# RWKV mixer: 128x128 matmuls over two heads in place of matmuls of 64 rows or columns

## Chip, cores and metric

The kernel runs on one core of one Trainium2 chip. The metric is device time in microseconds (us), the median of the runs.

## What is computed

A decoder trunk of two layers over 256 tokens of width 2048, in fp32: layer 0 mixes with window attention and a state-space scan, layer 1 with RWKV-7, and each is followed by a squared-ReLU MLP. The change lies in RWKV-7, which has 32 heads of 64 channels:

```python
def rwkv7_scan(r, w, k, v, a, b):
    def step(S, inp):
        r_t, w_t, k_t, v_t, a_t, b_t = inp
        sa = jnp.einsum('bhvk,bhk->bhv', S, a_t)
        S = S * w_t[:, :, None, :] + sa[..., None] * b_t[:, :, None, :] + v_t[..., None] * k_t[:, :, None, :]
        return S, jnp.einsum('bhvk,bhk->bhv', S, r_t)
...
    y = rwkv7_scan(rh, hs(decay), kh, vh, -kk, kk * ah)
    mu = jnp.mean(y, axis=-1, keepdims=True)
    var = jnp.mean(jnp.square(y - mu), axis=-1, keepdims=True)
    y = ((y - mu) * lax.rsqrt(var + GN_EPS)).reshape(b_, L, D)
    y = hs(y * ln_w.astype(jnp.float32) + ln_b.astype(jnp.float32))
    bonus = jnp.sum(rh * kh * r_k.astype(jnp.float32), axis=-1, keepdims=True) * vh
    y = (y + bonus).reshape(b_, L, D).astype(dt_)
    return (y * g) @ w_o.astype(dt_)
```

## The kernel before

Projections are made of 128-wide output tiles (units). Each fp32 weight is split into a rounded half (hi, ScalarE, L463) and the rest (lo, VectorE, L468); a k tile then takes three single-pass matmuls of 256 tokens, hi with the input's two halves and lo with the first (L494 to L496). They go to PSUM tiles named pu, from SA (values) or SB (keys and the output projection).

`mixer1` (L1202) handles 16 pairs of heads, one head on partitions 0 to 63 and one on 64 to 127. The 256 tokens are cut into 4 chunks of 64. The scan over tokens becomes products within a chunk, the inverse of a triangular matrix I - N, and a state carried over the chunks. For each pair j these stages run as generators:

- `prep_a` makes decay and gate and the scaled keys and queries, AR (ar, from the left) and bk.
- `prep_b` (L1363) multiplies bk by ar for each head (64 rows, 128 columns, fp32, 8 matmuls per pair) and masks the blocks into N (nt), ar and G; it sends the diagonal blocks of N through DRAM and transposes bk into bkn (8 transposes of 64 rows).
- `blocks`, `substitute` (GpSimd) and `levels` (32x32 matmuls, ps_i) make the inverse Y.
- `values` makes v and its transpose in uv (4 transposes of 128 rows to 64 columns).
- `chunks` (L1514) runs over 4 chunks, for both heads: the right side pr (L1527), from the second chunk on the state's part of the output (L1531), a copy rhs (VectorE), the inverse times it (L1543), the copy into uv (ScalarE), the state's update pS (L1553) and the output's other part (L1556), and the new state in uv (VectorE). Each is two matmuls, one per head, with the second head's result on partitions 64 to 127; the outputs are 64 wide.
- `finish` (L1566) does the group norm, transposes (4 of 128 rows to 64 columns), and multiplies by the gate on GpSimd.
- `keys`, `mixed`, `partial`, `whole` copy the projections' results and feed the output projection.

The order in which every engine gets its instructions is set by `Streams` (L200): it takes from all generators, the projections' among them, the operation that could start first by planned durations (`eP`, `eA`, `eD`, `eG`: TensorE, ScalarE, VectorE, GpSimd). `eW` names the events that a stage has to follow; with them the rings of buffers are kept. The third argument of `eP` is a shape: the time of the first load and of the last matmul. The numbers by which `Streams` chooses, and the order of the projections' parts, are in `PRM`. Each engine then executes its list in order and waits on semaphores where operands are late.

PSUM banks: pu 2, ps_a, ps_b, ps_i and ps_c one each, ps_y 2. AR has 4 buffers, KT 4 (and 3 in K3), bkn and G 3, bk 1, uv 2.

Of the kernel before, what the change touches and what calls it, by code (L numbers as in the profile page):

```python
# [13 lines left out]
P = 128  # L14
D = 2048
# [30 lines left out]
def _consts():  # L46
# [24 lines left out]
    c["blk32"] = (s64 // 32) == np.arange(2)[None, :]  # L71
# [10 lines left out]
for _k, _v in CONST.items():  # L82
    _l = int(_k in ("triu", "cos", "sin", "amask"))     # the second array serves layer 0 alone
    COFF[_k] = (_l, NCONST[_l], _v.shape[1])
    NCONST[_l] += _v.shape[1]


def _units(w):
    """[K, M] -> [M/128, 128, K/128, 128]"""
    k, m = w.shape  # L90
    return np.ascontiguousarray(w.reshape(k // P, P, m // P, P).transpose(2, 1, 0, 3))
# [6 lines left out]
def _heads(v):  # L98
    """a column to a head, on the first 64 partitions"""
    return np.concatenate([v.reshape(-1, HD).T, np.zeros((HD, D // HD), np.float32)], 0)  # L100


def layout(inp):
# [55 lines left out]
# ---------------------------------------------------------------- interleaving  # L159

WIDE, TILES, COLS, SMALL = (0.107, 0.107), (0.053, 0.02), (0.107, 0.002), (0.027, 0.02)


def eP(cost, after=None, shape=WIDE):
    """shape: the time to load the first stationary operand, which the matmul before hides, and the
    last matmul's time, which hides the next load"""
# [23 lines left out]
# the order of the parts of the projections and the weights by which Streams chooses  # L190
# [1531 lines left out]
```

## Time and profile before

| what | before |
| --- | --- |
| median of 3 runs | 2543.54 us (2540.68 to 2544.55) |
| span of the profiled execution | 2551.5 us (its own time is not listed beside it) |
| instructions | 45990 |
| TensorE busy, share of the span | 2477.5 us, 97% |
| VectorE | 1738.2 us, 68% |
| ScalarE | 1306.5 us, 51% |
| GpSimd | 527.2 us, 21% |
| mean granted clock of TensorE | 0.983 |

The span runs from the first to the last instruction of one profiled execution. PE is TensorE, PEld its weight loads, DVE VectorE, ACT ScalarE, POOL GpSimd. Matmuls are pipelined, so the busy times of two that overlap aren't a sum of costs; the distance of starts is. In tile names, out<-in, buffer numbers are left out. 64*64 64x64 means 64 rows and 64 columns of the array, an operand of 64 partitions and 64 elements. An fp32 matmul stands as two records, a transpose or a projection's matmul as one. The mixer's pairs run from about 1285 to 1760 us.

### The profile page before, as it was taken

What the parts mean: (1) busy time and instruction counts of PE and PEld (TensorE: products, weight loads), DVE (VectorE), ACT (ScalarE), POOL (GpSimd) and SP (SyncE); (2) the same over time, 40 slices, a digit from 0 to 9 for tenths busy, and PEclk for the clock granted to TensorE, in tenths of its full rate; (3) what the DMA queues carried; (4) which work ended last, traced back from release to release, by engine and by line L of the source; (5) the groups of instructions that cost most, each with busy time, mean ns of one, the idle gap of its engine ahead of it and who ended that gap; (6) DMA issues with size and microseconds to landing.
All of it is one profiled execution on the core that took longest, in us unless ns stands there. A gap on an engine that the chain in (4) does not pass through costs nothing. (4 is left out here: it accounts for less than half of the span.)

```text
span 2551.5 us, 45990 instructions
## 1 busy us (share of the span) xinstructions
PE 2477.5 (97%) x17612; PEld 2181.3 (85%) x17612; DVE 1738.2 (68%) x3287; ACT 1306.5 (51%) x2398; POOL 527.2 (21%) x933
## 2 busy tenths in 40 slices
PE   8999999999999999979999999999899999999999
PEld 7988988888888888879998888788688888888887
DVE  7888876656656656679876767667665565665665
ACT  5455555435445345556656566555453453453543
POOL 3443200000000000046455656552200000000000
PEclk9999999999999999989999999899999999999999
DMA  5433455555555555634442323334455555555554
GB/s 193 141 108 109 151 187 182 187 185 188 184 189 184 188 184 188 209 113 164 162 153 93 108 95 106 97 108 171 145 190 186 187 184 188 185 188 185 189 194 162
DMA packets 130348, 415.27 MB, mean 163 GB/s; under 512 B 23600, under 2 KB 26288, under 8 KB 130128
## 3 DMA queue, kind: packets, MB, share of 16 engines
q1 hardware_dynamic: 128160, 406.44, 46.9%
q0 software_dynamic: 1968, 5.90, 0.6%
q8 instruction: 138, 2.26, 0.3%
q14 instruction: 82, 0.67, 0.1%
HBM read 407.56 MB, written 4.72 MB: 162 GB/s over the span
## 5 line engine op out<-in xcount | busy, mean ns | idle before, releaser
L322 DVE TENSOR_TENSOR lo<-wt,hi 128x1024 fp32r<-128x1024 f32 (+2 forms) x895 | 937.4, 1054 | 529.6 <-ACT hi L319 511.8
L319 ACT ACTIVATE hi<-wt 128x1024 fp32r<-128x1024 f32 (+2 forms) x945 | 813.6, 873 | 818.3 <-PE pu L343 786.7
L343 PE MATMUL pu<-SA,hi 128*128 128x512 f32 (+2 forms) x4184 | 1162.0, 349 | 18.2 <-ACT SA L319 8.0
L343 PE MATMUL pu<-SB,hi 128*128 128x512 f32 (+2 forms) x3304 | 1003.1, 366 | 4.0 <-POOL SB L322 2.2
L343 PE MATMUL pu<-SA,lo 128*128 128x256 f32 (+1 forms) x3168 | 895.8, 283 | 0.3 <-DVE lo L322 0.3
L343 PEld LDWEIGHTS pu<-SA,hi 128*128 128x128 f32 (+1 forms) x4184 | 724.8, 191 | 135.2 <-ACT hi L319 9.7
L343 PE MATMUL pu<-SB,lo 128*128 128x256 f32 x2752 | 775.7, 282 | 1.7 <-DVE lo L322 1.6
L343 PEld LDWEIGHTS pu<-SB,hi 128*128 128x128 f32 (+1 forms) x3304 | 587.0, 190 | 115.6 <-POOL SB L322 2.6
L343 PEld LDWEIGHTS pu<-SA,lo 128*128 128x128 f32 (+1 forms) x3168 | 603.6, 191 | 1.2 <-DVE lo L322 0.5
L343 PEld LDWEIGHTS pu<-SB,lo 128*128 128x128 f32 x2752 | 522.6, 190 | 2.5 <-DVE lo L322 2.3
L1694 POOL DMA_DIRECT2D out<-xT x16 | 8.7, 544 | 708.0 <-DVE xT L322 708.0
L1661 POOL DMA_DIRECT2D xd<-xh x13 | 7.2, 554 | 696.5 <-DVE xh L322 696.5
L322 DVE TENSOR_TENSOR xh<-xh,pu 128x256 f32<-128x256 f32 x164 | 69.2, 422 | 53.7 <-PE pu L343 51.1
L322 DVE TENSOR_TENSOR xT<-xT,pu 128x256 f32<-128x256 f32 x154 | 64.8, 421 | 47.9 <-PE pu L343 45.3
L322 POOL TENSOR_TENSOR lo<-wt,hi 128x512 fp32r<-128x512 f32 (+1 forms) x50 | 69.1, 1387 | 66.3 <-ACT hi L319 62.2
L322 POOL TENSOR_TENSOR xt<-Nb,X 128x60 f32<-128x60 f32 (+14 forms) x240 | 74.7, 311 | 28.4 <-DMA Nb<-dn 12.1
L322 POOL TENSOR_TENSOR X<-X,xt 128x60 f32<-128x60 f32 (+14 forms) x240 | 74.2, 309 | 16.4
L319 ACT ACTIVATE uv<-ps_c,n 64x64 f32<-64x64 f32 x128 | 39.5, 309 | 53.0 <-PE ps_c L343 40.3
L322 POOL TENSOR_TENSOR SB<-st,SB 128x256 fp32r<-128x256 f32 x44 | 49.3, 1135 | 43.8 <-ACT SB L319 31.4
L340 DVE SCALAR_TENSOR_TENSOR uw<-u,rb 128x256 f32<-128x256 f32 x128 | 54.5, 425 | 4.4
L340 DVE SCALAR_TENSOR_TENSOR st<-dx,vec,xh 128x256 f32<-128x256 f32 x80 | 53.3, 700 | 2.0 <-POOL SB L322 2.0
L322 DVE TENSOR_TENSOR u<-pu,eb 128x256 f32<-128x256 f32 x128 | 53.6, 418 | 0.0
(310 smaller groups left out, 2073.2 us busy)
## 6 DMA issues: line engine op xcount, KB each, us to landing
wt<-in_w_up SPq DMA_DIRECT2D x256, 512.0 KB
wt<-in_w_dn SPq DMA_DIRECT2D x256, 512.0 KB
wt<-in_w_in SPq DMA_DIRECT2D x64, 512.0 KB
wt<-in_w_out SPq DMA_DIRECT2D x32, 512.0 KB
wt<-in_w_k SPq DMA_DIRECT2D x32, 512.0 KB
wt<-in_w_v SPq DMA_DIRECT2D x32, 512.0 KB
wt<-in_w_o SPq DMA_DIRECT2D x32, 512.0 KB
wt<-in_w_r SPq DMA_DIRECT2D x26, 512.0 KB
```

The costliest lines, as they stand in the source:

```text
L319: return self.nc.scalar.activation(out=out, in_=in_, func=func, **kw)
L322: return (eng or self.nc.vector).tensor_tensor(out=out, in0=a, in1=b, op=op)
L340: return self.nc.vector.scalar_tensor_tensor(out=out, in0=a, scalar=s, in1=b, op0=op0, op1=op1)
L343: return self.nc.tensor.matmul(out, lhsT, rhs, start=start, stop=stop)
L1661: spill = lambda d, e=nc.gpsimd: e.dma_start(out=xd[:, d, :], in_=x[d])
L1694: store = lambda d: nc.gpsimd.dma_start(out=ap["out"][:, d, :], in_=x[d])
```

## The change

In `chunks`, `prep_b`, `values` and `finish`, matmuls and transposes use all 128 rows and columns. AR holds for each head 128 columns: the scaled keys with what prep_b puts on the other half of the partitions, and the queries, with zeros elsewhere; one product (L1527's) then gives the right side on one half of the partitions and the state's part of the output on the other. BG holds the transposed bk and G together, so that a second product gives the state's update and the output's other part. `finish` adds the two parts of the output (R, the copy of the first product, and ps_y). Y becomes block diagonal over both heads, and one matmul of 128 columns replaces two. prep_b's 8 matmuls are issued head by head in turn into two banks. `Streams` gets a further number per shape, the rows, and plans 0.09 us where it changes. `_heads` repeats ln_w and ln_b on both halves. ps_b gets 2 banks, used in turns by prep_b and finish (`claim`), ps_y 1; AR 3 buffers, KT 3. `PRM` stays. Comments are removed; the diff shown leaves them out.

```diff
-WIDE, TILES, COLS, SMALL = (0.107, 0.107), (0.053, 0.02), (0.107, 0.002), (0.027, 0.02)
+WIDE, HALF, COLS, SMALL, ROWS = (0.107, 0.107, 128), (0.107, 0.053, 128), (0.107, 0.002, 128), (0.027, 0.02, 32), (0.107, 0.107, 64)
...
-            return max(self.free["P"] + max(0.0, load - self.tail), t + load - 0.07)
+            drain = 0.0 if op[3][2] == self.rows else 0.09
+            return max(self.free["P"] + drain + max(0.0, load - self.tail), t + load - 0.07)
...
-            AR = [wk.tile([P, 4, 3, HD], F32, name=f"AR{i}") for i in range(4)]
+            AR = [wk.tile([P, 4, 2, 2, HD], F32, name=f"AR{i}") for i in range(3)]
-            YY = [wk.tile([P, 4, HD], F32, name=f"YY{i}") for i in range(2)]
+            YY = [wk.tile([P, 4, 2, HD], F32, name=f"YY{i}") for i in range(2)]
+            for ar in AR:
+                for i in range(2):
+                    nc.gpsimd.memset(ar[H[1 - i], :, i, 1 - i, :], 0.0)
... prep_a
-                yield eW(("w", ("l", j, 0)), ("keys", j), ("chunks", j - 4), ("values", j - 2),
-                         ("finish", j - 4))
+                yield eW(("w", ("l", j, 0)), ("keys", j), ("values", j - 2), ("finish", j - 4))
...
+                yield eW(("chunks", j - 3))
...
-                yield eG(0.69, 0)
-                self.mul(ar[:, :, 1, :], v4(r), EE[:, :, 1:], nc.gpsimd)
+                for i in range(2):
+                    yield eG(0.69, 0)
+                    self.mul(ar[H[i], :, i, 1 - i, :], v4(r)[H[i]], EE[H[i], :, 1:], nc.gpsimd)
...
-                yield eG(0.69, t_kq)
-                self.mul(bk[:, :, 1, :], v4(kq), IE[:, :, 1:], nc.gpsimd)
+                for i in range(2):
+                    yield eG(0.69, t_kq)
+                    self.mul(bk[H[i], :, 1 - i, :], v4(kq)[H[i]], IE[H[i], :, 1:], nc.gpsimd)
... prep_b
+                turn = yield from claim()
+                pb = [PT("ps_b", 2) for _ in range(2)]
+                t_P = yield eP(0.9, None, ROWS)
+                for cc in range(4):
+                    for i in range(2):
+                        self.mm(pb[i][:, cc * P:(cc + 1) * P], bk[H[i], cc], ar[H[i], cc, i])
                 for i in range(2):
-                    ps = PT("ps_b")
-                    t_P = yield eP(0.87)
-                    for cc in range(4):
-                        self.mm(ps[:, cc * P:(cc + 1) * P], bk[H[i], cc, i:i + 2, :], ar[H[i], cc, i:i + 2, :])
...
-                for i in range(2):
-                    ps = PT("ps_b")
-                    yield eP(0.22, t_G[-1] if i == 0 else None, TILES)
-                    for cc in range(4):
-                        self.tp(ps[:, cc * HD:(cc + 1) * HD], bk[H[i], cc, i:i + 2, :], c["ident"][H[i], H[i]])
-                    yield eA(0.26)
-                    self.act(bkn[:, :, i, :], v4(ps[:, 0:L]))
+                ps = PT("ps_b", 2)
+                yield eP(0.48, t_G[0])
+                for cc in range(4):
+                    self.tp(ps[:, cc * P:(cc + 1) * P], bk[:, cc].rearrange("p s d -> p (s d)"), c["ident"])
+                done["ps_b", turn] = yield eA(0.47)
+                self.act(BG.rearrange("p c i s d -> p c (i s) d")[:, :, 0:4:3, :], ps.rearrange("p (c i d) -> p c i d", c=4, d=HD))
... values (finish alike)
-                for cc in range(4):
-                    self.tp(ps[0:HD, cc * P:(cc + 1) * P], v[:, cc * HD:(cc + 1) * HD], c["ident"])
+                yield eG(0.15, 0)
+                nc.gpsimd.memset(uv[:, 0], 0.0)
+                t = yield eP(0.25)
+                for a in range(2):
+                    self.tp(ps[:, a * P:(a + 1) * P], v[:, a * P:(a + 1) * P], c["ident"])
-                for i in range(2):
-                    t = yield eA(0.26, t if i == 0 else 0)
-                    self.act(uv[H[1 - i], :, i, :], pv[0:HD, :, i, :])
+                for n in range(4):
+                    i, b = n // 2, n % 2
+                    t = yield eA(0.24, t if n == 0 else 0)
+                    self.act(to[H[1 - i], :, b, i, :], pv[H[b], :, i, :])
... levels
-                self.mul(Y.rearrange("p c (q t) -> p c q t", q=2), two(Xt), sel("blk32", 32))
+                self.mul(Y.rearrange("p c h (q t) -> p c (h q) t", q=2), Xt.unsqueeze(2).broadcast_to([P, 4, 4, 32]),
+                         c["blk32"].unsqueeze(1).unsqueeze(3).broadcast_to([P, 4, 4, 32]))
... chunks
-                yield eW(("levels", j), ("values", j), ("finish", j - 2))
+                yield eW(("levels", j), ("values", j), ("y", j - 1))
-                    t = yield eP(0.13, t_S, TILES)
-                    for i in range(2):
-                        k = H[1 - i] if cc == 0 else slice(0, P)
-                        self.mm(pr[H[i], 0:HD], ar[k, cc, 2 * i, :], uv[k, cc, i, :])
-                    if cc:
-                        yield eP(0.13, t_S, TILES)
-                        for i in range(2):
-                            self.mm(yp[H[i], q], ar[H[i], cc, 1, :], uv[H[i], cc, i, :], True, False)
+                    t = yield eP(0.45, t_S, HALF)
+                    for i in range(2):
+                        self.mm(pr[:, i * HD:(i + 1) * HD], ar[:, cc, i], uv[:, cc, i, :])
...
-                    nc.vector.tensor_copy(rhs, pr[:, 0:HD])
+                    nc.vector.tensor_copy(R[:, cc], pr[:, 0:P].rearrange("p (i d) -> p i d", d=HD))
-                    t = yield eP(0.13, t_r, TILES)
-                    for i in range(2):
-                        self.mm(pu[H[i], 0:HD], Y[H[i], cc, :], rhs[H[i]])
+                    t = yield eP(0.23, t_r)
+                    self.mm(pu[:, 0:P], Y[:, cc], R[:, cc])
...
-                            self.mm(pS[H[i], 0:HD], bkn[:, cc, i, :], uv[:, cc, i, :])
-                    yield eP(0.13, t_u, TILES)
+                    t = yield eP(0.45, max(t0, t_u), HALF)
                     for i in range(2):
-                        self.mm(yp[H[i], q], G_[:, i, cc, :], uv[:, cc, i, :], cc == 0, True)
+                        self.mm(py[:, cc, i, :], BG[:, cc, i], uv[:, cc, i, :])
... finish
+                yv = yc = T("yc", 1, [P, 4, HD])
+                for i in range(2):
+                    o = H[1 - i]
+                    t = yield eD(0.34, 0 if i else None)
+                    self.add(yv[o], py[o, :, i, :], q_["R"][o, :, i, :])
+                done[("y", j)] = t
```

## Rows read from the trace of the kernel before

**Rows 1.** Busy by stretch: us; PE, PEld, DVE, ACT, POOL (records); clock; DMA; GB/s

```profile
1285.00:1760.00 475.00, 459.34 (x5193) 395.82 (x5191) 336.34 (x982) 282.20 (x704) 273.21 (x653) 0.95 0.35 114
```

**Rows 2.** By tile: ns min/median/max, first and last start in us, forms

```profile
L343 PE MATMUL ps_y<-uv,G x256: 222/222/314, 1341.9 to 1748.5; 128*64 128x64 f32 x128
...
L322 DVE TENSOR_TENSOR AR<-ka,EE x32: 402/422/1237, 1276.9 to 1678.1; 64x256 f32<-64x256 f32 x32
```

**Rows 3.** TensorE's timeline: start us, us to last end, operation, records

```profile
1502.59 1.16 PE L343 MATMUL ps_b<-AR,bk 64*128 64x128 f32 x8
1503.68 0.34 PE L343 MATMUL ps_c<-uv,bkn 128*64 128x64 f32 x4
1503.84 0.29 PE L343 MATMUL ps_y<-uv,G 128*64 128x64 f32 x4
1504.06 0.63 PE L346 MATMUL pu<-cst,v 128*64 128x128 f32 x4
1504.44 0.48 PE L343 MATMUL pu<-SB,hi 128*128 128x256 f32 x2
1504.76 0.28 PE L343 MATMUL pu<-SB,lo 128*128 128x256 f32 x1
1504.97 0.34 PE L343 MATMUL ps_c<-uv,AR 128*64 128x64 f32 x4
1505.23 0.33 PE L343 MATMUL ps_y<-uv,AR 64*64 64x64 f32 x4
...
1505.84 0.28 PE L343 MATMUL pu<-SB,lo 128*128 128x256 f32 x1
...
1506.55 0.28 PE L343 MATMUL ps_a<-hid,ll 96*128 96x256 f32 x1
1506.76 0.33 PE L343 MATMUL ps_c<-rhs,YY 64*64 64x64 f32 x4
1507.02 0.51 PE L343 MATMUL pu<-SB,hi 128*128 128x256 f32 x2
1507.36 0.29 PE L343 MATMUL pu<-SB,lo 128*128 128x256 f32 x1
1507.49 0.40 PE L343 MATMUL pu<-SB,hi 128*128 128x256 f32 x2
1507.72 0.28 PE L343 MATMUL pu<-SB,lo 128*128 128x256 f32 x1
```

**Rows 4.** The same timeline around a group of transposes

```profile
1591.99 0.48 PE L343 MATMUL pu<-SB,hi 128*128 128x256 f32 x2
1592.31 0.28 PE L343 MATMUL pu<-SB,lo 128*128 128x256 f32 x1
1592.52 0.46 PE L346 MATMUL ps_b<-cst,bk 64*128 64x64 f32 x4
...
1593.25 0.29 PE L343 MATMUL pu<-SB,lo 128*128 128x256 f32 x1
```

**Rows 5.** Timeline of the weight loads, four for the norm of k

```profile
1509.96 0.53 PEld L343 LDWEIGHTS ps_a<-cst,k 128*128 128x128 f32 x4
```

**Rows 6.** VectorE by operation and shape, 1285 to 1760: busy us, mean ns

```profile
L1539 DVE COPY rhs<-ps_c 128x64 f32<-128x64 f32 x64 | 14.2, 222 | 15.3 <-PE ps_c L343 14.0
...
L322 DVE TENSOR_TENSOR NT<-ps_b,NT 64x256 f32<-64x256 f32 x32 | 13.5, 421 | 15.6 <-PE ps_b L343 12.7 <-issue 1.5 <-POOL xt L322 0.5
...
L322 DVE TENSOR_TENSOR YY<-Xt,cst 128x256 f32<-128x256 f32 x16 | 6.9, 433 | 0.5
...
L322 DVE TENSOR_TENSOR Pm<-ps_i,cst 128x128 f32<-128x128 f32 x16 | 4.6, 289 | 2.5 <-PE ps_i L343 2.3
```

**Rows 7.** ScalarE, the same view

```profile
L319 ACT ACTIVATE ysq<-ps_y,vec 64x256 f32<-64x256 f32 x32 | 18.0, 561 | 10.8 <-PE ps_y L346 10.2
```

**Rows 8.** GpSimd, the same view

```profile
L322 POOL TENSOR_TENSOR bk<-k,Lc 128x256 f32<-128x256 f32 x15 | 11.8, 788 | 7.6 <-PE ps_b L346 7.0
```

**Rows 9.** TensorE's longest wait, 1285 to 1760: us in total, times, longest

```profile
PE ps_i L343 <- DVE Pm L322: 3.0, 4, 1.4
```

More of the change, by code (lines that the diff above doesn't have):

```diff
@@ L70, in _consts @@
     c["blk16"] = (s64 // 16 % 2) == np.arange(2)[None, :]
-    c["blk32"] = (s64 // 32) == np.arange(2)[None, :]
+    c["blk32"] = (r[:, None] // 32) == np.arange(4)[None, :]
     c["i16"] = (r % 16)[:, None] == np.arange(16)[None, :]
@@ L98, in _heads @@
 def _heads(v):
-    return np.concatenate([v.reshape(-1, HD).T, np.zeros((HD, D // HD), np.float32)], 0)
+    return np.concatenate([v.reshape(-1, HD).T] * 2, 0)
 def layout(inp):
@@ L216, in __init__ @@
         self.last = 0.0
-        self.tail = WIDE[1]
+        self.tail, self.rows = WIDE[1:]
         self.dma = 0.0
@@ L278, in run @@
                 if eng == "P":
-                    self.tail = h[1][3][1]
+                    self.tail, self.rows = h[1][3][1:]
                 self.free[eng] = t + cost
@@ L1218, in mixer1 @@
             self.ts(dv[:, 4, :], self.vcol("k_k", 0, 16), -1.0, ALU.mult)
-            AR = [wk.tile([P, 4, 3, HD], F32, name=f"AR{i}") for i in range(4)]
+            AR = [wk.tile([P, 4, 2, 2, HD], F32, name=f"AR{i}") for i in range(3)]
             NT = [wk.tile([P, 4, HD], F32, name=f"NT{i}") for i in range(3)]
-            YY = [wk.tile([P, 4, HD], F32, name=f"YY{i}") for i in range(2)]
-            KT = [self.K3[:, i, :] for i in range(3)] + [wk.tile([P, L], F32, name=f"KT{i}") for i in range(4)]
+            YY = [wk.tile([P, 4, 2, HD], F32, name=f"YY{i}") for i in range(2)]
+            KT = [self.K3[:, i, :] for i in range(3)] + [wk.tile([P, L], F32, name=f"KT{i}") for i in range(3)]
             dn = [self.dr.tile([8, 16, 4, 16], F32, name=f"dn{i}") for i in range(2)]
@@ L1312, in prep_a @@
                 ps = PT("ps_a")
[L1313 removed]
+                t_n = yield eP(1.1, max(t_k2, t_ta), COLS)
                 lora(ps[:, 0:L], [(2, P, hg[:, 0, :]), (3, P, hg[:, 1, :])])
@@ L1508, in levels @@
                         self.mm(v5[lo_[h], cc, 0:32], P5[hi_[h], cc, :], Xt[hi_[h], cc, :])
[L1509 to L1512 removed]
+                for h in range(2):
+                    yield eA(0.16, t)
+                    self.act(Y[lo_[h], :, h, 32:], v5[lo_[h], :, 0:32])
             def chunks(j):
                 q_ = ctx[j]
[L1517 to L1519 removed]
+                yield eW(("levels", j), ("values", j), ("y", j - 1))
+                ar, BG, uv, Y, dC, n2 = AR[j % 3], q_["BG"], q_["uv"], YY[j % 2], q_["dC"], q_["n2"]
+                yp = q_["yp"] = PT("ps_y")
+                py = yp.rearrange("p (c i d) -> p c i d", c=4, d=HD)
+                R = q_["R"] = T("R", 1, [P, 4, 2, HD])
                 t_S = 0
                 for cc in range(4):
[L1522 removed]
                     pr = PT("ps_c")
[L1524 removed]
+                    t = yield eP(0.45, t_S, HALF)
                     for i in range(2):
[L1526 to L1531 removed]
+                        self.mm(pr[:, i * HD:(i + 1) * HD], ar[:, cc, i], uv[:, cc, i, :])
                     if 0 < cc < 3:
@@ L1603, in finish @@
                 self.mul(yc, yc, y.unsqueeze(2).broadcast_to([P, 4, HD]), nc.gpsimd)
-                ps = yp
-                yield eP(0.43)
-                for cc in range(4):
-                    self.tp(ps[0:HD, cc * P:(cc + 1) * P], yc[:, cc, :], c["ident"])
-                yo = T("ysq", 1, [P, 4, HD]).rearrange("p a d -> p (a d)")
-                pv = ps.rearrange("p (c h t) -> p c h t", h=2, t=HD)
-                for i in range(2):
-                    yield eA(0.45, sch.last if i == 0 else 0)
-                    self.act(v4(yo)[H[i]], pv[0:HD, :, i, :], AF.Identity, scale=self.vcol("ln_w", 2 * j + i)[0:HD],
-                             bias=self.vcol("ln_b", 2 * j + i)[0:HD])
+                turn = yield from claim()
+                ps = PT("ps_b", 2)
+                yield eP(0.25)
+                for a in range(2):
+                    self.tp(ps[:, a * P:(a + 1) * P], yc[:, 2 * a:2 * a + 2, :].rearrange("p c d -> p (c d)"), c["ident"])
+                yo = T("ysq", 1, [P, 4, HD]).rearrange("p a d -> p (a d)")
+                pv = ps[:, 0:L].rearrange("p (a h t) -> p a h t", h=2, t=HD)
+                to = yo.rearrange("p (a b t) -> p a b t", b=2, t=HD)
+                for n in range(4):
+                    i, b = n // 2, n % 2
+                    t = yield eA(0.35, sch.last if n == 0 else 0)
+                    self.act(to[H[i], :, b, :], pv[H[b], :, 1 - i, :], AF.Identity, scale=self.vcol("ln_w", 2 * j + i)[H[b]],
+                             bias=self.vcol("ln_b", 2 * j + i)[H[b]])
+                done["ps_b", turn] = t
                 yield eG(0.69)
```

56 lines of the change are left out of this document (23 added, 33 removed).

## The prediction, made before the changed kernel was run

> **What bounds the kernel now.** I read three views in this order. First the table of busy time by stretch, for the stretch in which the pairs of heads run, 1285 to 1760 us [rows 1]: TensorE is busy for 459.3 of 475 us, VectorE for 336.3 (71%), ScalarE for 282.2 (59%), GpSimd for 273.2 (58%). So TensorE sets the pace there, and it is idle for only 15.7 us. The granted clock of 0.95 says that about a tenth of the stretch ran at 1.2 GHz rather than 2.4 GHz, which costs at most 24 us. Outside this stretch the diff changes no operation of the kernel (only small memsets at the head of the mixer, where TensorE doesn't need GpSimd), so the whole difference comes from here. Second, the instructions by tile [rows 2]: they give the counts (128 matmuls on G, eight per pair, stand as 256 records, so an fp32 matmul is two), and how the pairs follow one another: the scaled keys of pair 0 are written at 1276.9 us and the last of pair 15 at 1678.1 us, so a pair takes (1678.1 - 1276.9) / 15 = 26.7 us. Third, TensorE's timeline around one chunk [rows 3, 4]. The reader is to see starts, not durations, because records overlap: what a group of small matmuls costs is the time by which the next start of the projection's stream is put off.
>
> **What a group of small matmuls costs now.** The stream alone takes 0.36 us for three records (1507.36 to 1507.72), 0.12 us each [rows 3]. From the single record ahead of a group of four 64x64 records (1506.55) to the single lo behind it (1507.36) there are 0.81 us, of which 0.36 is the stream's: 0.45 us. Of that the switch into the small form is 0.08 us (0.21 from lo to the group rather than 0.13), and the rest is the group and the way back: the two hi records behind it take 0.34 us (1507.02 to 1507.36) rather than 0.23 (1507.49 to 1507.72). Two groups of different forms in a row, 128*64 then 64*64, cost 1505.84 - 1504.76 - 0.36 = 0.72 us. Two groups of the same form, 128*64, take 0.16 and 0.22 us to the next start (1503.68, 1503.84, 1504.06); with 0.08 in and 0.10 out that is 0.57 us. The eight records of prep_b take 1.09 us (1502.59 to 1503.68), with 0.08 in and 0.10 out 1.27 us [rows 3]. A group of four transposes of 64 rows costs 1593.25 - 1592.31 - 0.36 = 0.58 us [rows 4]. Four transposes of 128 rows to 64 columns take 0.38 us (1504.06 to 1504.44), and need no switch.
>
> **Removed, per pair.** In chunks: the first product with the state's output behind it, three times 0.72 = 2.16, and once alone 0.45; the inverse, four times 0.45 = 1.80; the state's update with the output behind it, three times 0.57 = 1.71, and the last output alone 0.45. In prep_b 2 x 1.27 = 2.54 and 2 x 0.58 = 1.16. The transposes of values and finish 2 x 0.38 = 0.76. The sum is 11.0 us. Where two groups stand side by side, as at 1502.59 to 1504.06, they share a switch; I take 0.5 off for that: 10.5 us.
>
> **Added, per pair.** A product of 128 stationary columns and 64 moving ones isn't in the trace. The nearest row are the four loads for ps_a<-cst,k, 128x128 each with two moving columns: (0.53 - 0.19) / 3 = 0.113 us from load to load [rows 5]. So four records take 0.45 us, eight times per pair 3.6. The inverse over both heads, 128 moving columns, is two records: 0.24 us, four times 0.95. A group whose last matmul is short can't cover the next load: after that group of two columns hi to lo takes 0.32 us (1591.99 to 1592.31) instead of 0.23 [rows 4]; for 64 columns I take half of that, 0.05 x 8 = 0.4. prep_b becomes one group of 16 records in which the two heads alternate on different halves of the rows; that a second tile runs beside the first is seen in the four records at 1503.84, which last 0.29 us from the first start to the last end [rows 3], where one alone lasts 0.222 [rows 2]. So 1.09 + 0.08 + 0.10 + 0.06 = 1.33. Four full transposes at 0.113 are 0.45, and two each in values and finish 0.45 together. The sum is 7.2 us.
>
> Saved on TensorE: 10.5 - 7.2 = 3.3 us per pair, 16 x 3.3 = 53 us. The bounds: if a record with 64 columns goes at the pace of the small group (0.26 us for four), 1.5 us more per pair, 77 us in all; if it goes at prep_b's pace (1.09 / 8 = 0.136), 0.7 us less, and if the heads don't overlap in prep_b another 0.95 less, which leaves 53 - 11 - 15 = 27 us. I take 53, since a load per record is what the row shows.
>
> One rule of the Trainium skill speaks against this change. In these rows the tiles' own time is short and the switching is most of the price (0.08 in, 0.10 and more out, against 0.16 between two groups of one form) [rows 3]. The Trainium skill, TensorE: Matmul & The Clock Gate, section "Part 3: Packing small matmuls — row/col tiling", says to put small matmuls on separate tiles so that they run at the same time, which is what the kernel does now; the Trainium skill, TensorEngine Tiling (Array Packing), "Key Properties", adds that a change of tiling mode drains the engine. By the first alone the change loses; the rows agree with the second.
>
> **What moves to the other engines.** VectorE: the copy of the right side goes from 128x64 (222 ns) to 128x128 (289 ns as the product Pm) [rows 6], 64 x 0.067 = 4.3 us; finish gains two sums of 64x256 out of PSUM at 421 ns, 32 x 0.42 = 13.5 us; the masked Y doubles from 433 ns, at most 16 x 0.43 = 6.9, I take 5. Together 23 us: 336 becomes 359. ScalarE: the evictions in finish (561 ns [rows 7]) and in values are each cut in two; at no cost for the cut 0, at full cost for each piece at most 4 x 0.56 x 16 = 36 us, I take 12; the two of bk become one. GpSimd: two products per pair are issued by halves of partitions, and one (788 ns [rows 8]) costs between half and all of itself per half, 0 to 25 us, and a memset; I take 25: 273 becomes 298. The memset of uv is queued on GpSimd ahead of the substitution of a pair, and waits for the chunks two pairs before; by 58% busy I cost it at nothing, 0.8 us per pair if that cover is gone.
>
> None of these alone would hold the stage over 438 us, but they take back some of the gain. Nearly every wait of TensorE there ends on VectorE, as the longest [rows 9]. With a stage of 438 us VectorE's share rises from 0.71 to 0.82. As an estimate, waiting grows as share over rest: 0.71/0.29 = 2.4, 0.82/0.18 = 4.6, so 15.7 us of idle become about 30. I put 16 us for that with its share of half clock. **Forecast: 53 - 16 = 37 us less.** The span of the profiled execution is 2551.5 us, its own time isn't listed apart; the median of the runs is 2543.5, 8 us below the span. The sum is a difference within the span, and I take it off the median: 2507 us.
>
> **Waits that come and go.** AR has 3 buffers in place of 4, and prep_a's writing of it waits for the chunks three pairs before; behind it on VectorE stand all later steps. KT has 6 buffers in place of 7, and the copies of k that wait for them stand on ScalarE only. ps_y has one buffer: the chunks of the next pair wait for the two sums in finish, some 0.9 us behind the last matmul, hidden by the levels of the next pair. ps_b is shared by prep_b and finish in turns, so finish's transposes may wait until prep_b's copy is out; projections stand behind them on TensorE.
>
> **Rivals.**
> (a) VectorE and the order of issue take all of it. The numbers by which Streams chooses stay, and VectorE's steps are planned shorter than they run (0.34 us for 0.42). If VectorE's 359 us ran at the same 97% as TensorE does now the stage would be 370, so the bound itself isn't there; but if TensorE waits 45 us more, the time is 2535 to 2548. Chance 0.12.
> (b) The ring of pairs becomes the pace, and the kernel slower. Pair 15 writes its keys at 1678.1 and ends its last output at 1748.5 [rows 2]: 70 us, over three buffers 23.4 us per pair, under 26.7. Each chunk's own chain gets longer, since two products take 0.45 rather than 0.26 and the copy 0.07 more: some 0.5 x 4 = 2 us. It decides from 3 x 26.7 = 80 us on. If the shared ps_b puts 13 us on that way, it is 85 us, 28.3 per pair, 15 x 1.6 = 24 us slower: 2568. For it: this way is made of waits on four engines. Against it: these 70 us hold waiting for a busy TensorE, which shrinks. Chance 0.10.
> (c) The small groups cost only their own time, and switches are hidden. Then before is 18 x 0.16 + 2 x 1.09 + 2 x 0.39 + 0.76 = 6.6 us per pair against 7.2: 10 us slower, 2553. The 0.45 and 0.72 us of rows 3 speak against it. This is what the packing rule of the Trainium skill (TensorE: Matmul & The Clock Gate, Part 3) would give. Chance 0.03.
> (d) The heads don't overlap in prep_b, or a record takes 0.136 us: 27 us on TensorE, less 10 given back: 2526. Chance 0.15.
> (e) The forecast, 2470 to 2520: chance 0.60.
>
> **How the numbers follow.** The likeliest is (e), 2507. The range is 2470 (77 us on TensorE, 4 given back) to 2550, which takes in (d) and nearly all of (a) and leaves out (b), (c) and the ends. A measurement of this kernel can tell 0.2%, 5 us, from no change. Faster by more: (e), (d) and a fifth of (a), 0.77; within: 0.09; slower: (b), (c) and a little of (a), 0.14.
>
> **What would show it.** In the profile after, the stretch of the pairs should be near 438 us, with TensorE's busy time near 400. Its timeline should have starts of four records 0.45 us apart with no 0.21 us ahead of them, prep_b's 16 records in about 1.1 us, and lo to hi undisturbed. VectorE should be busy for 355 to 365 us. Wrong would be: prep_b in 1.9 us (d); TensorE idle for more than 50 us, ended by VectorE (a); prep_a's writing of AR right behind the chunks of three pairs before, and over 26.7 us per pair (b); groups of four at over 0.5 us.

## The result, and the profile after

The changed kernel takes 2697.0 us in the median (2688.5 to 2701.2) against 2542.7 us, a ratio of 1.061 [1.058, 1.064]: 154 us slower, where 2507 us was forecast. It lies outside the range. The span is 2694.2 us at a mean granted clock of 0.936, where before had 2551.5 us and 0.983.

The page of the changed kernel first: engines' busy time with share and instructions, then TensorE's row and its clock in the 40 slices.

```profile
PE 2524.3 (94%) x16972; PEld 2247.0 (83%) x16972; DVE 1769.5 (66%) x3319; ACT 1323.0 (49%) x2446; POOL 562.1 (21%) x987
...
PE   8999999999999999799888888788799999999999
...
PEclk9999999999999999899976778677899999999999
```

Slices 20 to 29 hold the stage of the pairs. TensorE shows 7s and 8s there, and its clock falls to 6 to 8 tenths. The stage itself, by the table of busy time by stretch (length; busy us with instructions of PE, PEld, DVE, ACT, POOL; granted clock; DMA share; GB/s), which answers to [rows 1]:

```profile
1285.00:1905.00 620.00, 504.69 (x4538) 456.97 (x4537) 367.06 (x1012) 298.30 (x752) 302.23 (x699) 0.76 0.27 87
```

It takes 620 us in place of 475, and the 145 us between them are the loss (the two profiled spans differ by 143). TensorE is busy for 45 us more although its work got less, and idle for 115 in place of 16. The clock of 0.76 says that 2 x 0.24 x 620 = 298 us of it ran at 1.2 GHz, against 48 before. The instructions by tile, which answer to [rows 2]:

```profile
L345 PE MATMUL ps_c<-R,YY x128: 270/421/583, 1349.6 to 1892.8; 128*128 128x128 f32 x128
...
L324 DVE TENSOR_TENSOR AR<-ka,EE x32: 406/423/1086, 1275.9 to 1792.8; 64x256 f32<-64x256 f32 x32
...
L345 PE MATMUL ps_y<-uv,BG x256: 217/421/477, 1350.5 to 1894.3; 128*128 128x64 f32 x128
```

A pair takes (1792.8 - 1275.9) / 15 = 34.5 us, where it took 26.7. The chunks' new products show a median of 421 ns where the shortest are 217 and 270: more than half of them run at the low clock. TensorE's timeline shows how the time goes (start, us, operation, records, in brackets the idle time before and what ended it). First a stretch of the projections:

```profile
1388.44 0.40 PE L345 MATMUL pu<-SB,hi 128*128 128x256 f32 x2
1388.68 0.28 PE L345 MATMUL pu<-SB,lo 128*128 128x256 f32 x1
...
1390.54 0.28 PE L345 MATMUL pu<-SB,lo 128*128 128x256 f32 x1
1393.08 0.44 PE L348 MATMUL pu<-cst,v 128*128 128x128 f32 x2 [2.26 <-DVE bv L324]
1393.45 0.45 PE L345 MATMUL ps_i<-X,NT 32*32 32x32 f32 x32
```

The operand X of that last group was written by VectorE at 1377.8 us, as this row of its tile in the same stretch says:

```profile
L1496 DVE STREAM_TRANSPOSE X<-Xt x1: 311/311/311, 1377.8 to 1377.8; 128x128 f32<-128x128 f32 x1
```

So the operand of the first product of `levels` was ready for 15 us while projections went ahead of it, and just before its turn TensorE stood still for 2.26 us: the next instruction of its list waited for VectorE's bv, and no projection had been put there. The other side of it, in the same timeline, is a chunk somewhat earlier:

```profile
1358.22 0.80 PE L345 MATMUL ps_c<-R,YY 128*128 128x128 f32 x2 [0.45 <-DVE R L1558]
1359.48 1.11 PE L345 MATMUL ps_y<-uv,BG 128*128 128x64 f32 x4 [0.46 <-ACT uv L321]
1360.96 1.12 PE L345 MATMUL ps_c<-uv,AR 128*128 128x64 f32 x4 [0.37 <-DVE uv L342]
1362.53 0.79 PE L345 MATMUL ps_c<-R,YY 128*128 128x128 f32 x2 [0.45 <-DVE R L1558]
```

No record of the projections stands between the steps, where in [rows 3, 4] several stand behind each group. Each step waits for the one before it, 4.3 us per chunk, at the low clock. Three stretches of 10 us around it, in the table of busy time by stretch (columns as above):

```profile
1350.00:1360.00 10.00, 8.02 (x88) 6.51 (x87) 3.38 (x11) 4.04 (x13) 5.06 (x20) 0.53 0.17 58
1360.00:1370.00 10.00, 7.74 (x27) 5.76 (x26) 5.69 (x21) 3.24 (x10) 3.08 (x11) 0.50 0.01 2
...
1380.00:1390.00 10.00, 9.91 (x80) 9.60 (x80) 7.30 (x14) 7.30 (x17) 3.60 (x6) 1.00 0.32 106
```

27 TensorE records in 10 us at 1.2 GHz, and hardly any weights are fetched (DMA share 0.01). The stage alternates between stretches full of projections and stretches in which a chain stands alone.

**The account.** I counted TensorE's records of the stage one by one, from 1285 us to the end of GpSimd's last write of RY: the spacing to the next record, less the idle time, halved where the clock was 1.2 GHz, is an estimate of the work at full clock. The kernels below the second are explained with their experiments.

| kernel | stage, us | idle | at 1.2 GHz | work at full clock |
| --- | --- | --- | --- | --- |
| before | 475.3 | 16.4 | 44 | 437.6 |
| after | 620.1 | 115.9 | 302 | 389.4 |
| e1_nodrain | 514.4 | 70.8 | 120 | 392.9 |
| e4_b_drain | 601.2 | 86.4 | 310 | 387.1 |
| e10_retuned | 482.5 | 47.7 | 87 | 395.1 |
| e8_b_nolo | 487.2 | 39.9 | 188 | 356.5 |
| e9_nodrain_more | 515.7 | 55.2 | 81 | 428.0 |
| e14_fill_beside | 613.0 | 90.9 | 141 | 467.8 |

From before to after the work fell by 48 us, idle time rose by 100, and the lower clock added (620.1 - 115.9 - 389.4) - (475.3 - 16.4 - 437.6) = 93 us: together the 145.

### The profile page after: what moved, and what is told of

It is laid out like the page before. It is cut to its first block, busy times and chain, and to the rows that moved or that the text cites. A ratio compares the mean times of both kernels' runs of the same rounds, so it can differ in the third digit from the quotient of the medians.

```text
span 2694.2 us, 44914 instructions
## 1 busy us (share of the span) xinstructions
PE 2524.3 (94%) x16972; PEld 2247.0 (83%) x16972; DVE 1769.5 (66%) x3319; ACT 1323.0 (49%) x2446; POOL 562.1 (21%) x987
## 4 chain that ended last, share of the span: by engine, by line
PE 77%; DVE 11%; issue 4%; POOL 3%; ACT 3%; DMA 1%; SPq 0%; POOLq 0%; DVEq 0%; ACTq 0%
PE pu L345 68%; PE ps_c L345 2%; DVE lo L324 2%; PE ps_y L345 2%; DVE st L342 1%; PE ps_t L345 1%; ACT ysq L321 1%; ACT uv L321 1%; POOL X L324 1%; PE ps_a L345 1%; POOL xt L324 1%; POOL xT L324 1%; PE ps_i L345 1%; PE ps_b L345 1%; DVE AR L324 0%
## 5 line engine op out<-in xcount | busy, mean ns | idle before, releaser
L345 PE MATMUL pu<-SB,hi 128*128 128x512 f32 (+2 forms) x3304 | 993.1, 364 | 8.8 <-ACT uv L321 4.7
L345 PEld LDWEIGHTS pu<-SA,hi 128*128 128x128 f32 (+1 forms) x4184 | 732.8, 193 | 137.4 <-ACT SA L321 12.7
L324 POOL TENSOR_TENSOR X<-X,xt 128x60 f32<-128x60 f32 (+14 forms) x240 | 79.8, 333 | 15.4
L345 PE MATMUL ps_y<-uv,BG 128*128 128x64 f32 x256 | 60.8, 381 | 14.1 <-ACT uv L321 14.0
L345 PEld LDWEIGHTS ps_y<-uv,BG 128*128 128x128 f32 x256 | 52.1, 281 | 24.8 <-ACT uv L321 23.9
L345 PE MATMUL ps_c<-uv,AR 128*128 128x64 f32 x256 | 58.6, 372 | 8.4 <-DVE uv L342 6.7
L345 PEld LDWEIGHTS ps_c<-uv,AR 128*128 128x128 f32 x256 | 51.4, 279 | 13.8 <-DVE uv L342 10.5
```

What stands on the lines that cost most here:

```text
L324: return (eng or self.nc.vector).tensor_tensor(out=out, in0=a, in1=b, op=op)
L345: return self.nc.tensor.matmul(out, lhsT, rhs, start=start, stop=stop)
```

## Experiments: the price in the choice

The diff also changes how `Streams` plans. It gives each shape a number of rows (128, 64 or 32), and a TensorE step whose number differs from that of the step before starts 0.09 us later in the plan. A projection behind a projection has no such price, so when both are ready the projection comes first, unless a weight of the stages says otherwise.

**e1_nodrain**, the changed kernel without it:

```diff
-            drain = 0.0 if op[3][2] == self.rows else 0.09
+            drain = 0.0
```

> The changed kernel with one number altered: Streams plans 0.0 us instead of 0.09 us where the rows of TensorE's tiles change. No instruction is added or removed; only the order of issue differs. Theory A (order of issue: the 0.09 us make every step on 32 or 64 rows start later than a projection's step that is always ready, so Streams puts them off, and the engines then wait for them in their fixed order): most of the 154 us go, 2500 to 2560 us, levels back to 7 to 10 us per pair from 7 to 30, TensorE idle in the stretch of the pairs under 50 us. Theory B (three buffers of AR and the shared ps_b make the ring of pairs the pace, whatever the order): 2660 to 2700 us, AR still written within 1 us behind the chunks of three pairs before, 33 to 35 us per pair.

2598.7 us, ratio 1.021 [1.019, 1.024]. One number in the planner is 98 of the 154 us. That is most of the loss, as theory A said, but the time lies over its range of 2500 to 2560 us, and TensorE idles for 71 us, not under 50. The stage in the table of busy time by stretch, its columns as above:

```profile
1285.00:1800.00 515.00, 444.18 (x4543) 409.52 (x4541) 370.13 (x1014) 297.94 (x754) 310.64 (x699) 0.88 0.35 105
```

**e2_choice** keeps the 0.09 us in the planned times and takes it out of the comparison alone:

```diff
                 b = t + (h[3]() if callable(h[3]) else h[3])
+                if h[1][0] == "P" and h[1][3][2] != self.rows:
+                    b -= 0.09
```

> The changed kernel, with the 0.09 us left in the planned times but taken out of the comparison by which Streams chooses the next step. Theory A in its narrow form (the harm comes from the choice, not from the planned times): like the run without the number, within 20 us of it, 2500 to 2560 us. If the planned times themselves do the harm (other steps are planned around them): 2640 to 2700 us. Theory B: 2660 to 2700 us.

2590.1 us, 1.018 [1.014, 1.022]: like e1_nodrain, and like it over the 2560 us of theory A. The harm is in what is chosen first, not in the planned time.

**e4_b_drain** is the opposite: the kernel before, all its 64-wide products as they were, with the numbers of rows and the 0.09 us alone.

```diff
-WIDE, TILES, COLS, SMALL = (0.107, 0.107), (0.053, 0.02), (0.107, 0.002), (0.027, 0.02)
+WIDE, TILES, COLS, SMALL, ROWS = (0.107, 0.107, 128), (0.053, 0.02, 64), (0.107, 0.002, 128), (0.027, 0.02, 32), (0.107, 0.107, 64)
...
+            drain = 0.0 if op[3][2] == self.rows else 0.09
```

> The kernel before with the planner's new term alone: shapes carry 128, 64 or 32 rows, and 0.09 us are planned where these differ. All operations, buffers and rings as before. Theory A: the loss appears without any of the new matmuls, 2620 to 2720 us, with levels stretched to 15 to 30 us for many pairs and more of the stretch at the lower granted clock. Theory B: within 1% of before, 2520 to 2570 us.

2681.5 us, 1.054 [1.050, 1.058]: 139 us slower without one new product, with the same picture in its row of busy time by stretch:

```profile
1285.00:1890.00 605.00, 518.59 (x5171) 448.71 (x5171) 337.26 (x981) 284.29 (x702) 271.74 (x651) 0.74 0.28 89
```

Most of the loss is the order, shown from both sides. The table of the account adds something: with the very products of before it counts 387 us of work where before has 438. With the price in the choice, products of one form stand together, and in the traces TensorE's records change their form (rows*columns) 390 times in this stage instead of 645. So an order alone took 50 us of work off TensorE, as much as the new products were to save, and the kernel became 139 us slower.

## Experiments: the ring and the planned durations

**e3_b_ring3**: the kernel before with the shorter rings, and prep_a's writing of AR behind the chunks of three pairs before.

```diff
-            AR = [wk.tile([P, 4, 3, HD], F32, name=f"AR{i}") for i in range(4)]
+            AR = [wk.tile([P, 4, 3, HD], F32, name=f"AR{i}") for i in range(3)]
...
+                yield eW(("chunks", j - 3))
```

> The kernel before with the rings of the change alone: AR 3 buffers in place of 4, KT 3 tiles in place of 4, and prep_a's writing of AR behind the chunks of three pairs before. All matmuls, ps_b and ps_y as before. Theory B: it shows a good part of the loss, 2590 to 2700 us. Theory A: 2540 to 2565 us, since the ring costs only what the plan already holds.

2558.9 us, 1.005 [1.003, 1.008]: some 14 us.

**e5_nodrain_ar4**: e1_nodrain with four AR buffers (their room from tiles that are free by then).

```diff
-            AR = [wk.tile([P, 4, 2, 2, HD], F32, name=f"AR{i}") for i in range(3)]
+            AR = [wk.tile([P, 4, 2, 2, HD], F32, name=f"AR{i}") for i in range(4)]
...
-                yield eW(("chunks", j - 3))
+                yield eW(("chunks", j - 4))
```

> e1_nodrain with the ring of AR at 4 buffers again (prep_a writes it behind the chunks of four pairs before). The room for it comes from tiles that are dead in this stage: two KT tiles stand in acc and rb, dv in columns of vec that only layer 0 reads, ka in th's tile, P5 in Pm's. In e1_nodrain AR was written 0.8 to 2 us behind the chunks of three pairs before in eight of 13 pairs, and its time is 56 us over the kernel before. Theory B2 (what is left of the loss is the ring of AR): 2545 to 2575 us. Theory C (what is left is that VectorE, ScalarE and GpSimd run longer than planned while TensorE now runs as planned, so that TensorE's fixed list waits for them): 2585 to 2605 us, TensorE idle as in e1_nodrain, near 70 us in the stretch of the pairs.

2592.7 us, 1.019 [1.016, 1.022]: 6 us under e1_nodrain, with intervals that overlap. The ring of AR is not what is left.

**e6_choice_prices** is e2_choice with longer planned durations, nearer to the measured ones, **e7_choice_prices_ar4** the same with four AR buffers.

```diff
+                cost *= self.mult.get(eng, 1.0)
...
+            sch.mult = {"D": 1.3, "A": 1.2, "G": 1.3}
```

> e2_choice, where in this stage Streams plans VectorE's steps at 1.3, ScalarE's at 1.2 and GpSimd's at 1.3 times its numbers: the sums of the planned steps against the busy times of the trace of before (262 planned, 350 busy; 240, 292; 214, 280). Rings as in the change. Theory C: TensorE's idle time in the stretch falls from 70 to under 45 us, and the time to 2540 to 2575 us. Theory B2: the ring holds it, 2580 to 2605 us.

> Both: the prices of e6_choice_prices and the four buffers of AR of e5_nodrain_ar4. If B2 and C each hold a part: 2520 to 2555 us, under both. If only one of them counts, within 8 us of the better of e5_nodrain_ar4 and e6_choice_prices.

2617.9 us, 1.028 [1.024, 1.032], and 2585.7 us, 1.015 [1.012, 1.018]. Better prices don't help by themselves: with three buffers the time is longer than that of e2_choice and over the ranges of both theories, with four it is 7 us shorter than e5_nodrain_ar4.

**e10_retuned** adds to e7_choice_prices_ar4 weights of the stages and an order of the projections' parts chosen anew for the new steps; **e15_order_115** and **e16_order_100** are two further choices, with smaller factors on the planned durations and with none.

```diff
+PRM.update({'w_blocks': -1.533, 'order': ['v0a', 'l0a', 'l1a', 'v0b', 'k3a', 'v1a', 'k3b',
...
'w_substitute': -0.001, 'w_finish': -0.109, 'step2': 1, 'w_chunks': -0.122, 'w_partial': 0.743, 'w_keys': -0.083, 'b2p': 0.002})
```

> The changed kernel with the switch price kept out of the choice, the longer planned durations of the other engines and four AR buffers as in e7_choice_prices_ar4 (2585.7 us), and beside that the weights of the stages and the order of the projections' parts in PRM chosen anew for the 128x128 products. Theory R (what is left over the kernel before after e7 is that PRM was fitted to the old steps): the stage of 499 us falls to the neighbourhood of the 475 us of before or under it, 2540 to 2565 us. Theory L (the dependent steps of a pair have got longer, and no order takes that back): 2570 to 2590 us.

> As e10_retuned (2562.3 us), with the weights and the order of the parts chosen further, and the planned durations of VectorE and GpSimd 1.15 times the kernel's own in place of 1.3 (ScalarE 1.1 in place of 1.2). Theory R (what is over the kernel before is the order alone): 2525 to 2555 us. Theory L (the new steps are longer in a chain, and the order can't take that back): 2555 to 2580 us.

> As e15_order_115, chosen with the kernel's own planned durations. Theory R: 2525 to 2555 us. Theory L: 2555 to 2590 us; over e15_order_115 if the planned durations matter, since VectorE's steps run longer than these.

2562.3 us, 1.007 [1.005, 1.010]; 2569.7 us, 1.008 [1.005, 1.011]; 2582.0 us, 1.013 [1.010, 1.016]. The stage of e10_retuned, busy time by stretch:

```profile
1285.00:1768.00 483.00, 435.34 (x4574) 403.79 (x4572) 364.19 (x1017) 300.01 (x757) 309.58 (x700) 0.91 0.37 113
```

With the same products, a new order and a fourth AR buffer are worth 135 of the 154 us, and the buffer's share was 6 us in e5_nodrain_ar4. None of the three gets under the kernel before. The stage of e10_retuned has 42 us less work than that of before, and pays them back with 31 us more idle time and 18 us of lower clock. (These profiles put its stage 7 us over that of before; by the medians the kernel is 19 us slower, since the profiled span of before lies 9 us over its median.) The first held to the upper end of theory R, the other two fell to theory L. That no better order exists is not shown, so whether the longer chain or the order keeps the rest stays open. The single ps_y and the shared ps_b, which the change brought too, were not run apart from the rest.

## Experiments: what sets the length of the stage

**e8_b_nolo** is the kernel before, in its own order, without the third product (lo) of the projections of this stage.

```diff
+                    less = p.unit[0] in ("v", "o", "o+") or p.unit[0] == "k" and p.unit[1] > 2
...
+                    if not less:
+                        self.mm(ps, lo[:, kk], p.X[:, k, 0:L], False, k == p.end - 1)
```

> The kernel before, with the third matmul of each k tile (lo times the input's first half) left out of the projections of this stage (k from the fourth on, v, the output projection's first half): 616 matmuls of 0.12 us, 74 us of TensorE's work, in the same order of issue with the same plan; these products lose that term. Theory P (TensorE's work is the bound of the stage, as the prediction had it): 2470 to 2495 us. Theory D (the chains of dependent steps in their fixed order are as long as the stage; what is taken off TensorE becomes idle time, and idle time becomes half clock): 2510 to 2550 us, with TensorE idle for 50 to 90 us instead of 16 and the lower clock for over 90 us instead of 44.

2566.8 us, 1.010 [1.007, 1.013]. The page of the profile has 672 matmuls less than that of before (the 616 of the expectation are too few), and 607 of them are missing in the stage. With 607 x 0.12 = 73 us less of TensorE's work there the kernel is slower, by more than either theory allowed (theory D ended at 2550 us). Its stage, busy time by stretch:

```profile
1285.00:1772.00 487.00, 448.25 (x4586) 369.97 (x4586) 330.34 (x972) 278.43 (x696) 272.34 (x650) 0.81 0.35 108
```

TensorE is still busy for 448 us of 487, at a clock of 0.81. At the lower clock each record takes longer, and so most of the work that was taken away stands in the busy time again. By the table of the account, 81 us less work came with 24 us more idle time, where theory D had expected 34 to 74, and 70 us more for the lower clock.

**e9_nodrain_more** is e1_nodrain, in its own order, with more projection products of 0.12 us, into columns that nobody reads: 420 in the kernel by the pages of the profiles (385 were expected), 324 of them in the stage, 39 us.

```diff
+                    if kk < 5 and p.n == 8 and (p.unit[0] in ("v", "o", "o+") or p.unit[0] == "k" and p.unit[1] > 2):
+                        self.mm(sums[p.unit][:, L:], hi[:, kk], p.X[:, k, 0:L], False, k == p.end - 1 or False)
```

> e1_nodrain with work added to TensorE alone: five more matmuls of 0.12 us in each half of a projection of this stage, into the unread half of its PSUM bank; 385 matmuls, 46 us, about what the change takes off, in the same order of issue with the same plan. Theory P: 2635 to 2650 us. Theory D: 2585 to 2612 us, that is within 0.5% of e1_nodrain, with less idle time and less time at the lower clock.

2601.0 us, 1.024 [1.020, 1.029], where e1_nodrain has 2598.7 us and 1.021 [1.019, 1.024]: the added work cost 2 us by the medians and 7 by the ratios, neither clear of the intervals. The time at 1.2 GHz fell from 120 to 81 us, and the busy time rose by 17 us (x4867 records where e1_nodrain has x4543):

```profile
1285.00:1801.00 516.00, 461.00 (x4867) 432.82 (x4866) 368.04 (x1008) 295.35 (x748) 307.85 (x696) 0.92 0.34 104
```

**e11_b_longer** makes the copy of the right side three times in the first three chunks of each pair in the kernel before, where the inverse's product waits for it; **e12_b_beside** puts as many copies where no product of the chain waits.

```diff
                     nc.vector.tensor_copy(rhs, pr[:, 0:HD])
+                    for _ in range(2 if cc < 3 else 0):
+                        nc.vector.tensor_copy(rhs, pr[:, 0:HD])
```

```diff
                                 self.stt(uv[h, cc + 1, i, :], pS[h, 0:HD], dC[h, cc:cc + 1], ALU.mult, SD[h], ALU.add)
+                        for _ in range(2):
+                            nc.vector.tensor_copy(rhs, yp[:, q])
```

> The kernel before, in its own order, where the copy of the right side in the first three chunks of each pair is made three times into the same place: 96 more copies of 222 ns that the inverse's product has to wait for, 21.3 us of VectorE's work, none of TensorE's. Theory C (the chain of dependent steps sets the length of the stage): slower by 12 to 30 us, 2555 to 2573 us, with as much more idle time of TensorE. Theory T (TensorE's work sets it, the projections fill the gap): within 5 us of before.

> The kernel before, in its own order, with as many copies of the same shape (96, from PSUM, some 21 us of VectorE's work) placed behind the new state of the first three chunks of each pair, into a place that nobody reads, so that the next product of the chain doesn't wait for them. Theory C (the chain sets the length): a third or less of what e11_b_longer costs, 0 to 8 us slower. If VectorE's amount of work set it, as much as e11_b_longer, 12 to 30 us. Theory T (TensorE's work sets it): within 5 us of before in both.

1.0029 [1.0004, 1.0054] and 1.0030 [1.0009, 1.0051]: both some 7 us, a third of the 21 us added, whatever the place. Theory C missed for the copies in the chain: the chunks' chain does not by itself set the length of the kernel before either. The 5 us of theory T lie inside both intervals, so T is not refuted here; e8_b_nolo refutes it. As far as these runs go, the order has slack around the chunks, and no one resource is the bound that an amount of work could be set against.

**e13_fill** is the changed kernel with products that nobody reads, behind the groups of a chunk, to keep TensorE busy while it waits; **e14_fill_beside** moves them to banks that the next copy does not read.

```diff
+                    self.mm(pr[:, 256:512], c["ident"], self.cst[:, 0:256])
...
+                    self.mm(pu[:, 256:512], c["ident"], self.cst[:, 0:256])
```

```diff
+                    for _ in range(2 if cc < 3 else 0):
+                        self.mm(py[:, 3].rearrange("p i d -> p (i d)"), c["ident"], self.cst[:, 0:P])
...
+                    self.mm(pu[:, 256:512], c["ident"], self.cst[:, 0:256])
```

> The changed kernel (2697.0 us), in its own order, with one more fp32 product of 128x128 by 256 columns right behind each of the three groups of a chunk, into columns of the bank that nobody reads: 192 products more, 0.43 us each at 2.4 GHz by the row of pu<-rk,rkb (two records, 1439.54 to 1439.97 in e1_nodrain), 83 us of TensorE's work, none for the other engines. They stand where TensorE waits 0.4 to 0.6 us for VectorE or ScalarE. Theory K (idle time between the steps brings the 1.2 GHz level, and that level costs most): the time at 1.2 GHz in the stage falls from 302 us to under 200 and the whole rises by less than half of the 83 us or falls, 2620 to 2735 us. Theory W (the waiting on the other engines costs, and the clock only accompanies it): the time at 1.2 GHz stays over 250 us and the whole rises by 50 to 120 us, 2745 to 2820 us.

> As e13_fill (2752.5 us), but with the added products where nothing has to wait for them. In e13_fill they wrote the bank that VectorE and ScalarE were to read next, and the records show that the copies waited for them (the next group 0.45 us behind the end of the added one), so the added time stood in the chain itself and the run told little. Here the two gaps ahead of the copies take two products of 128 columns each (0.24 us each) into a part of the output's bank that is written later, and the gap ahead of the new state one of 256 columns (0.43 us) into a bank that has been read: 74 us of TensorE's work, 4.6 us per pair. Theory K (idle time brings the 1.2 GHz level, and that level costs most): the time at 1.2 GHz in the stage is under 200 us (302 in the changed kernel) and the whole 2580 to 2690 us, under the changed kernel's 2697. Theory W (the waiting costs and the clock only accompanies it): 2700 to 2770 us, whatever the clock shows.

2752.5 us, 1.084 [1.078, 1.089], and 2698.2 us, 1.062 [1.059, 1.066]. In the first the copies waited for the fill. Its time lies in the range of theory W (2745 to 2820 us), but its 226 us at 1.2 GHz lie between the two theories (under 200, over 250), and with the fill in the chain itself it settles nothing. The second has the changed kernel's time to 0.2% with 74 us more work on TensorE. Its stage, busy time by stretch:

```profile
1285.00:1898.00 613.00, 522.60 (x5024) 474.96 (x5022) 363.61 (x1008) 294.47 (x744) 298.07 (x695) 0.88 0.28 87
```

And a chunk in its timeline, where the added records (ps_c<-cst, ps_y<-cst) stand between the steps:

```profile
1358.06 0.77 PE L345 MATMUL ps_y<-uv,BG 128*128 128x64 f32 x4 [0.40 <-ACT uv L321]
1358.67 0.65 PE L345 MATMUL ps_c<-cst 128*128 128x256 f32 x2
1359.15 0.56 PE L345 MATMUL ps_c<-uv,AR 128*128 128x64 f32 x4
1359.78 0.71 PE L345 MATMUL ps_y<-cst 128*128 128x128 f32 x4
```

The clock is 0.88 in place of 0.76, and the time at 1.2 GHz 141 us in place of 302: work between the steps brings more than half of the lost full clock back, as theory K said. But the kernel is no faster, since the fill took what the clock gave: by the table of the account 78 us more work, 25 us less idle time and 60 us less for the lower clock. The run ended between the two theories' ranges: it shows that the low level hangs on what TensorE is given to do between the steps, and not how many of the 93 us would return if the clock alone were mended.

## Why the prediction was wrong

Two steps failed: the first explains why no gain came in any order that was tried, the second, larger in time, why most of the loss came.

**The first failed step: "So TensorE sets the pace there".** It was read from a busy share of 97% [rows 1]. A busy share that high can also be a schedule in which the gaps between dependent steps were filled with projections, and the runs fit this: taking some 73 us of that filling away made the kernel 1.0% slower (e8_b_nolo), and adding 39 us to e1_nodrain (e9_nodrain_more) or 74 us to the changed kernel (e14_fill_beside) cost nothing that the runs can tell. Freed time on TensorE became idle time and low clock. The Trainium skill, Perfetto Trace Analysis, section "Identifying the Most-Contended Engine", calls the matmul busy share a poor measure of how close a kernel is to its roofline and names, beside the share of peak arithmetic, that of the weight loads; in [rows 1] that is 395.8 of 475 us, 83%, the highest of the other rows, and would have named the same engine.

**The second failed step: "The numbers by which Streams chooses stay", in rival (a).** The diff changes them: the rows and the 0.09 us stand in it, and I gave that part no cost. It holds 98 us (e1_nodrain) to 139 us (e4_b_drain), more than every term that I did work out. Rival (a) has the right mechanism, the order of issue, and was stopped at the time of before only because I let it take back the gain and no more.

**The terms of TensorE's sum were of the right size.** Saved on TensorE: 53 us forecast; 437.6 - 392.9 = 45 counted in e1_nodrain and 42 in e10_retuned, whose choices hold no price of a switch. The 48 us of the changed kernel can't be put down to the products alone, since e4_b_drain counts 50 us less than before with the old ones. Their prices, in e1_nodrain's timeline at full clock:

```profile
1285.92 1.16 PE L345 MATMUL ps_b<-AR,bk 64*128 64x128 f32 x16
...
1401.18 0.28 PE L345 MATMUL pu<-SA,lo 128*128 128x256 f32 x1
1401.30 0.56 PE L345 MATMUL ps_y<-uv,BG 128*128 128x64 f32 x4
1401.66 0.48 PE L345 MATMUL pu<-SA,hi 128*128 128x256 f32 x2
1401.98 0.29 PE L345 MATMUL pu<-SA,lo 128*128 128x256 f32 x1
```

From lo to the group 0.12 us, not 0.21: no switch. The group and the way back take 1401.98 - 1401.30 - 0.24 = 0.44 us, where 0.50 was forecast with its share of the next load. prep_b's 16 records take 1.16 us, so the heads overlap (8 take as long in [rows 3]), and rival (d) falls with rival (c). The packing rule weighed in the prediction does not decide here. The Trainium skill, TensorEngine Tiling (Array Packing), section "Key Properties", says that a change of tiling mode drains TensorE; 0.12 us against 0.21 agrees. VectorE came to 367 us (359 forecast), ScalarE to 298 (282 + 12), GpSimd to 302 (298).

**The give-back was mis-sized: 16 us forecast, 193 counted** (100 idle, 93 clock). Without the price in the choice it is still 84 us in e1_nodrain and 50 in e10_retuned, more than the work saved. The estimate from VectorE's share, 15.7 to 30 us, knew nothing of order. Where the waits end speaks for order too; TensorE's waits of the changed kernel in the stage (who waited for what: us in total, times, longest), where [rows 9] has 3.0 us as the longest group of before's `levels`:

```profile
PE ps_c L345 <- DVE R L1558: 20.6, 38, 1.7
PE pu L348 <- DVE bv L324: 16.3, 12, 2.8
PE ps_y L345 <- ACT uv L321: 14.0, 32, 0.7
PE ps_i L345 <- DVE X L1496: 9.3, 5, 4.3
```

The first and the third are many and short and stand on the chain of the chunks; the second is ahead of the transposes of values, the fourth in `levels`. They end at engines that are busy for 59% and 48% of the stage: nobody is overloaded, the steps stand alone.

**Rival (b) showed its sign without being the cause.** A pair took 34.5 us, and in 9 of 13 pairs VectorE wrote AR 0.8 us behind the end of the chunks of three pairs before, as (b) says. But e4_b_drain loses 139 us with all its four buffers, the shorter ring costs 14 us in the kernel before (e3_b_ring3), and a fourth buffer gives at most some 6 us back (e5_nodrain_ar4).

## What to carry over

A high busy share doesn't show that an engine is the bound: before a saving on it is turned into time, ask what would fill the freed slots, or take some of its work away without changing the order and see whether the time falls. In a kernel whose order a greedy planner makes, every number that enters its choice is a part of the change with a price of its own; a price per switch sends the many cheap steps ahead of the few that a chain waits for. Retune the order before judging the new instructions.

## What the runs showed of the hardware

Idle time on TensorE came with between half as much and as much again in clock: 31 us more of it than in before with 18 us in e10_retuned, 54 with 29 in e1_nodrain, 100 with 93 in the changed kernel. With 16 us of idle time the stage of before had 44 us at 1.2 GHz, e10_retuned 48 and 87, the changed kernel 116 and 302. It isn't the idle time alone: e8_b_nolo had 40 us of it and 188 us at 1.2 GHz, so work taken out of the stream came back as slower work. And 74 us of products that nobody reads, put into waiting time, raised the clock from 0.76 to 0.88 at no cost in time (2698.2 us against 2697.0), although the idle time fell only from 116 to 91 us. Nor is fewer changes of form a gain by itself: with 390 of them in place of 645 in the stage, e4_b_drain was 139 us slower.
